# A two-layer encoder on one core: the first norm completed ahead of the projections, and projection tiles convolved straight from PSUM

## The chip, the cores and the metric

One core of a Trainium2 chip runs the whole program. The metric is the time of one execution in microseconds on the device; lower is better. The kernel before was timed three times: median 1426.7 us, from 1426.19 to 1429.39.

## What is computed

The reference is a trunk of two layers over 528 positions (16 learned tokens and 512 inputs) of width 1024. Both layers have the same shape: norm, mixer, norm, residual.

```python
for i in range(DEPTH):                       # DEPTH = 2
    y = rmsnorm(h, norm_pre[i])              # x * rsqrt(mean(x*x) + 1e-6) * gain
    y = hyena_mixer(...) if i == 0 else diff_attention_mixer(...)
    h = h + rmsnorm(y, norm_post[i])
return h[:, 16:]

def hyena_mixer(h, ...):                     # layer 0, inner width E = 2048
    u = h @ w_in + b_in                      # 1024 -> 4 * 2048: x0, x1, v and the gate z
    x0, x1, v = split(dwconv_centred(u[..., :3 * E], conv_w, conv_b))   # three taps
    h_fwd, h_bwd = hyena_filters(...)        # a small sine net, then 64 -> 2 * 2048
    v = bidir_long_conv(v * x1, h_fwd, h_bwd, skip)
    return (v * x0 * silu(u[..., 3 * E:])) @ w_out
```

Layer 1 is differential attention with 16 heads. Everything is float32; a product of two float32 matrices is made of three products of a rounded high part and the rest (high by high, high by low, low by high).

## The kernel before

**Layout.** Activations lie transposed, 1024 channels as 8 blocks (`KT`) of 128 partitions by 528 positions. `xh` and `xl` hold the high and low parts of the normed input of a layer. A weight tile (`wtile`, L325) is loaded in two halves of 128x512 through three buffers `wr`; for each half ScalarE writes the high part `wh` (L209) and VectorE or GpSimd the low part `wl` (L212).

**Layer 0.** Its 2048 channels go in 8 chunks of 256. In a chunk there are eight projection tiles (`in_tile`, L487): v, x1, v, x1, then x0, z, x0, z. A tile is 48 matmuls of 264 columns (`project`, L338: 8 blocks, three products, two halves of the positions). Beside them stand the filters (`filters`, L596: for each chunk `taps`, `tap_sums` and `tap_transform` twice), which need the three-layer sine net `filter_net` (L581) to be complete, then for each chunk the long convolution (`long_conv`, L713) and eight tiles of the output projection (`out_tile`, L855; `out_half` for the last two chunks).

**The first norm.** In `first_load` (L448) `xh` and `xl` are made from x times gain, without the norm's factor, so that projections may start at once. The squares are summed over the blocks on VectorE (L465), then over partitions on TensorE (L270), the root is made on VectorE (L220 to L231), and `first_norm` spreads the 528 factors over all partitions as `rb0`. Each projection tile is multiplied by `rb0` as it leaves PSUM (L504), into a tile `u`, from which ScalarE makes the centre tap (L519) and VectorE the two others (L520, L521).

**PSUM.** Pool `psB` has five banks and `psP` three. A projection tile, two outputs of a filter transform (`tap_transform`) take two banks of `psP`; all else, the out tiles too, takes `psB`.

**What sets the order.** A list of steps (`Filler`) hands out projection and out tiles between the pieces of the filters and convolutions, and a list scheduler of the framework then fixes the order on each engine. Each engine runs its queue strictly in order. All loads go through the queue of SP.

## Time and profile before

| what | value |
|---|---|
| median of three runs | 1426.7 us |
| the profiled execution | 1425.88 us, its span 1424.1 us |
| TensorE busy | 1334.7 us, 94% of the span |
| VectorE busy | 1092.5 us, 77% |
| ScalarE, GpSimd busy | 737.6 us (52%), 568.8 us (40%) |
| mean granted TensorE clock | 0.974 |

The program runs through four stretches: the opening (first loads, first norm, sine net) to about 71 us, the filters to about 194 us, the convolutions to about 690 us, and then the second norm and the attention layer. Time that an engine sits idle counts only where another waits for it; with TensorE at 94%, the stretches where it is not dense are the ones to look at.

### The profile page before, as it was taken

How to read it: one execution, taken by the hardware profiler on the slowest of the kernel's cores; microseconds unless marked ns; L12 is line 12 of the kernel's file. 1: busy time of each engine (PE TensorE's matmuls, PEld its weight loads, DVE VectorE, ACT ScalarE, POOL GpSimd, SP SyncE). 2: the span in 40 equal slices, each digit the busy share in tenths (PEclk: the TensorE clock that was granted, in tenths of full speed). 3: DMA queues.
4: the chain of work that ended last, by engine and by line, in shares of the span. 5: the costliest groups of instructions: out<-in, count | busy, mean ns of one | idle time of the engine just before them, and what ended most of it. 6: DMA issues, size and time to landing. Idle time of an engine off the chain costs nothing. (4 is left out here: it accounts for less than half of the span.)

```text
span 1424.1 us, 24660 instructions
## 1 busy us (share of the span) xinstructions
PE 1334.7 (94%) x9296; PEld 1242.8 (87%) x9296; DVE 1092.5 (77%) x1972; ACT 737.6 (52%) x1415; POOL 568.8 (40%) x678
## 2 busy tenths in 40 slices
PE   5989999999999999999888999999999999899994
PEld 4888899999999999999887788897979889797983
DVE  8889988877777777767778676868678676867877
ACT  5455433443323232323447678665677666567662
POOL 7367634532323232322534244433444443344334
PEclk7999999999999999999988999999999999999997
DMA  5443442232323232323321412212121221212211
GB/s 188 135 138 123 148 153 75 75 119 75 104 75 104 74 105 69 102 72 97 111 61 34 133 46 75 63 42 80 40 89 60 72 68 39 75 45 89 90 67 59
DMA packets 63558, 123.47 MB, mean 87 GB/s; under 512 B 7296, under 2 KB 11648, under 8 KB 63440
## 3 DMA queue, kind: packets, MB, share of 16 engines
q1 hardware_dynamic: 63440, 121.91, 26.3%
q8 instruction: 73, 1.20, 0.4%
q14 instruction: 45, 0.37, 0.1%
HBM read 109.30 MB, written 12.58 MB: 86 GB/s over the span
## 5 line engine op out<-in xcount | busy, mean ns | idle before, releaser
L209 ACT CAST wh<-wr 128x512 fp32r<-128x512 f32 x314 | 182.1, 618 | 238.6 <-PE b L350 66.7
L350 PE MATMUL b<-xl,wh 128*128 128x264 f32 x1024 | 263.3, 289 | 4.8 <-DVE xl L460 4.8
L350 PE MATMUL b<-xh,wh 128*128 128x264 f32 x1024 | 264.9, 291 | 2.5 <-DVE ho L710 0.9
L350 PE MATMUL b<-xh,wl 128*128 128x264 f32 x1024 | 258.6, 289 | 0.8 <-POOL wl L212 0.8
L212 DVE TENSOR_TENSOR wl<-wr,wh 128x512 fp32r<-128x512 f32 x250 | 185.9, 774 | 34.9 <-ACT wh L209 33.4
L350 PEld LDWEIGHTS b<-xh,wh 128*128 128x128 f32 x1024 | 183.9, 193 | 6.3 <-DVE u L504 1.5
L350 PEld LDWEIGHTS b<-xl,wh 128*128 128x128 f32 x1024 | 183.7, 192 | 6.5 <-DVE xl L460 6.1
L350 PEld LDWEIGHTS b<-xh,wl 128*128 128x128 f32 x1024 | 181.6, 192 | 1.3 <-POOL wl L212 1.1
L212 POOL TENSOR_TENSOR wl<-wr,wh 128x512 fp32r<-128x512 f32 x64 | 94.9, 1500 | 62.0 <-ACT wh L209 61.9
L347 PE MATMUL b<-xh,wh 128*128 128x512 f32 x232 | 93.2, 402 | 6.9 <-DVE acc L1266 6.9
L1323 DVE TENSOR_REDUCE mx<-a 128x1 f32<-128x528 f32 x128 | 88.7, 699 | 9.7 <-PE a L1320 8.9
L347 PE MATMUL b<-xh,wl 128*128 128x512 f32 x232 | 91.7, 395 | 0.0
L347 PE MATMUL b<-xl,wh 128*128 128x512 f32 x232 | 91.6, 395 | 0.0
L1266 DVE SCALAR_TENSOR_TENSOR acc<-b,rh,acc 128x512 f32<-128x512 f32 x96 | 70.8, 743 | 22.8 <-PE b L1251 21.9
L516 POOL TENSOR_SCALAR u<-vecs 128x1 f32<-128x1 f32 x96 | 26.4, 296 | 151.6 <-DVE cv L521 129.5
L1329 POOL COPY pp<-pp 128x80 f32<-128x80 f32 x64 | 16.5, 257 | 166.5 <-DVE pp L1328 143.1
L1181 POOL TENSOR_TENSOR ro<-ro,rope 128x528 f32<-128x528 f32 (+1 forms) x32 | 43.2, 1350 | 79.2 <-ACT ro L1170 78.8
L1203 PE MATMUL b<-wh,xh 128*128 128x256 f32 x256 | 73.8, 288 | 0.4 <-DVE vl L1213 0.4
L1203 PE MATMUL b<-wl,xh 128*128 128x256 f32 x256 | 72.6, 284 | 0.0
L1203 PE MATMUL b<-wh,xl 128*128 128x256 f32 x256 | 72.3, 282 | 0.0
L212 DVE TENSOR_TENSOR pl<-b,ph 128x512 fp32r<-128x512 f32 x64 | 43.7, 685 | 33.2 <-ACT ph L209 32.5
L1317 PE MATMUL a<-ks,qs 128*128 128x264 f32 x256 | 55.2, 298 | 10.0 <-ACT qs L209 6.2
(391 smaller groups left out, 4027.3 us busy)
## 6 DMA issues: line engine op xcount, KB each, us to landing
wr<-in_w_in SPq DMA_DIRECT2D x128, 256.0 KB, 2.8
wr<-in_w_out SPq DMA_DIRECT2D x64, 256.0 KB, 2.8
hsp<-ho SPq DMA_DIRECT2D x16, 512.0 KB, 2.7
H<-hsp SPq DMA_DIRECT2D x16, 512.0 KB, 3.9
wr<-in_w_k SPq DMA_DIRECT2D x32, 256.0 KB, 2.7
wr<-in_w_q SPq DMA_DIRECT2D x32, 256.0 KB, 2.7
wr<-in_w_z SPq DMA_DIRECT2D x32, 256.0 KB, 2.7
wr<-in_w_v SPq DMA_DIRECT2D x32, 256.0 KB, 2.6
```

The source lines that it names most:

```text
L209: self.nc.scalar.copy(dst, src)
L212: (eng or self.nc.vector).tensor_tensor(dst, src, hi.bitcast(F32), op=ALU.subtract)
L347: te.matmul(ps, w[:, wk], x[:, k, first:T], start=st, stop=sp)
L350: te.matmul(ps[h], w[:, wk], x[:, k, h * TH:(h + 1) * TH], start=st, stop=sp)
L516: g.tensor_scalar(u[:, e:e + 1], b_in[:, mt:mt + 1], -1.0, None, op0=ALU.mult)
L1181: g.tensor_tensor(y, y, rope[:, 1, n0:n0 + n], op=ALU.mult)
L1203: te.matmul(ps[:n, :256], x, wv[k // 4][w][:, wk], start=(k == 0 and q == 0), stop=(k == KT - 1 and q == len(ops) - 1))
L1266: self.nc.vector.scalar_tensor_tensor(y, ps, r, y, op0=ALU.mult, op1=ALU.add)
L1317: te.matmul(pss[mp][:, h, :TH], qs[:, mp, tq], ks[:, mp, h * TH:(h + 1) * TH], start=True, stop=False)
L1323: v.tensor_reduce(mx, ps[:, :, :TH], axis=AX.XY, op=ALU.max, negate=True)
L1329: self.nc.gpsimd.tensor_copy(view(p, 0, [META, 5], [1, META]), view(p, MR - META, [0, 5], [1, META]))
```

## The change

Three things are done in the code. The first norm is completed before any projection: the squares of each block are summed over partitions on TensorE as they come (`sums`), the root is made with a power on GpSimd (`mhalf`), and each block is then scaled, rounded to `xh` and its rest written to `xl`, in a fixed order. The first two weight tiles are split on VectorE, and two projection tiles are worked on side by side. Projection tiles, now already normed, are convolved directly out of PSUM: `u`, `rb0` and the 264-column products are gone, six fixed tiles `cv` with a column of padding at each end take their place, and a small addition on GpSimd mends the two end columns. PSUM is cut into `psB` with four single banks and `psP` with two pairs; out tiles move to `psP`, and are added to the accumulator in one instruction of 528 columns. A halving of one tap row (L670) moves into a constant. The title of the change also speaks of the second layer's weights, split where they are used; the diff has no line for that, and on all five engines the instructions of the attention layer stand in the same order as before (the last 3641 of TensorE, 800 of VectorE, 699 of ScalarE, 330 of GpSimd, 188 of SP).

```diff
-        self.psB = px.enter_context(tc.tile_pool(name="ps0", bufs=5, space=PSUM))
-        self.psP = px.enter_context(tc.tile_pool(name="ps1", bufs=3, space=PSUM))
+        self.psB = px.enter_context(tc.tile_pool(name="ps0", bufs=4, space=PSUM))
+        self.psP = px.enter_context(tc.tile_pool(name="ps1", bufs=2, space=PSUM))
...
+            items[1], items[2] = items[2], items[1]
...
+                    xts, sums, net = self.first_load(pf, fill)
+                    layers = self.filter_net(pf, hs, net)
+                    next(layers)
+                    with tc.high_priority(offset=400):
+                        last = self.first_norm(pf, xts, sums)
...
+                    with tc.issue_after(last[0]), tc.issue_after(last[1]):
+                        fill.upto(4)
+                        for _ in layers:
+                            fill.upto(fill.at + 2)
+                        self.tables(pf, vb, nb, ib, hb)
...
     def first_load(self, pf, fill):
...
+        for i in (0, 1):
+            fill.fetch(i, nc.vector)
+        for k, xt in enumerate(xts):
             sq = self.tl(pf, [P, T], F32, "sqk", bufs=4)
             nc.scalar.activation(sq, xt, AF.Square)
+            for j in range(6):
+                nc.tensor.matmul(sums[:88, j:j + 1], sq[:, j * 88:j * 88 + 88], self.ones[:, 0:1],
+                                 start=k == 0 and j == 0, stop=k == KT - 1 and j == 5)
...
+    def first_norm(self, pf, xts, sums):
+        v, s, m = self.nc.vector, self.nc.scalar, 88
+        a, y, q, r = [self.tl(self.small, [P, 8], F32, t)[:m, :6] for t in ("rs_a", "rs_y", "rs_q", "rms")]
+        v.tensor_scalar(a, sums[:m, 0:6], 1.0 / D, 1e-6, op0=ALU.mult, op1=ALU.add)
+        self.nc.gpsimd.tensor_tensor(y, a, self.mhalf[:m, :6], op=ALU.pow)
+        v.scalar_tensor_tensor(q, y, -0.5, y, op0=ALU.mult, op1=ALU.mult)
+        v.tensor_tensor(q, q, a, op=ALU.mult)
+        v.scalar_tensor_tensor(r, q, 1.5, y, op0=ALU.add, op1=ALU.mult)
+        rb = self.tl(pf, [P, T], F32, "rb0")
         for h in (0, 1):
             ps = self.tl(self.psB, [P, 512], F32, "b")
+            self.rows(r, 3 * h, 3, m, ps[:, :TH])
+            s.copy(rb[:, h * TH:(h + 1) * TH], ps[:, :TH])
+        keep = self.tc.keep_in_program_order
+        for k in range(KT + 1):
+            if k < KT:
+                xt, xh = xts[k], self.xh[:, k]
+                keep(v.scalar_tensor_tensor(xt, xt, self.gains[:, 0, k:k + 1], rb, op0=ALU.mult, op1=ALU.mult))
+                cast = keep(s.copy(xh, xt))
+            if k:
+                low = keep(v.tensor_tensor(self.xl[:, k - 1], xts[k - 1], self.xh[:, k - 1].bitcast(F32), op=ALU.subtract))
...
     def in_tile(self, pa, b_in, cw, cb2, c, idx, wt, res, part):
...
+            res["ps", idx] = self.tl(self.psP, [P, 2, 512], F32, "b")
...
-                v.tensor_tensor(dst[:, sl], ps[h], self.rb0[:, sl], op=ALU.mult)
...
-        for e in (0, T + 1):
-            g.tensor_scalar(u[:, e:e + 1], b_in[:, mt:mt + 1], -1.0, None, op0=ALU.mult)
-        scaled(u[:, 1:T + 1])
-        s.activation(y, u[:, 1:T + 1], AF.Identity, bias=cb2[:, mt:mt + 1], scale=cw[:, 1, mt:mt + 1])
-        v.scalar_tensor_tensor(y, u[:, 0:T], cw[:, 0, mt:mt + 1], y, op0=ALU.mult, op1=ALU.add)
-        v.scalar_tensor_tensor(y, u[:, 2:T + 2], cw[:, 2, mt:mt + 1], y, op0=ALU.mult, op1=ALU.add)
+        s.activation(at(1), ps, AF.Identity, bias=cb2[:, mt:mt + 1], scale=cw[:, 1, mt:mt + 1])
+        for o in (2, 0):
+            v.scalar_tensor_tensor(at(o), ps, cw[:, 2 - o, mt:mt + 1], at(o), op0=ALU.mult, op1=ALU.add)
+        g.tensor_tensor(ends, ends, self.edge[:, mt], op=ALU.add)
...
-                v.tensor_scalar(pm[0:1, 0], pm[0:1, 0], 0.5, None, op0=ALU.mult)
...
     def out_tile(self, c, st, ws, dt):
-        pss = [self.tl(self.psB, [P, 512], F32, "b")[:, :TH] for _ in (0, 1)]
+        pair = self.tl(self.psP, [P, 2, 512], F32, "b")[:, :, :TH]
...
+            nc.vector.tensor_tensor(ya, ya, pair, op=ALU.add)
```

In numbers of instructions: VectorE loses 128 products of 264 columns (L504), 40 of its 80 out-tile additions (two of 264 become one of 528), 7 sums of squares and 8 halvings, and gains 6 weight splits and 8 subtractions (the 8 scaled rests become 8 scalings and 8 subtractions). GpSimd loses 96 single-column instructions and 6 splits and gains 48 end-column additions. TensorE gains 46 small products. The order on the engines moves at three places.

**VectorE, the first norm.** Before, the root (`rs_a`) stands behind the last sum of squares `sqk`, between two sine layers (`sa`, `sk`):

```order
L465 TENSOR_TENSOR sqk_148<-sqk_148,sqk_199 128x528
L535 TENSOR_SCALAR sa_235<-b_231,net_131 64x264
L465 TENSOR_TENSOR sqk_148<-sqk_148,sqk_206 128x528
L538 TENSOR_SCALAR sk_236<-sa_235 64x528
L212 TENSOR_TENSOR wl_451<-wr_452,wh_450 128x512
L539 TENSOR_SCALAR sk_236<-sk_236 64x528
L220 TENSOR_SCALAR rs_a_254<-b_247 88x6
```

Now the root stands directly behind the split of the fourth weight half (`wr_179`), and the scaled blocks `xt` and rests `xl` follow:

```order
L559 TENSOR_SCALAR sa_252<-sa_252 64x528
L213 TENSOR_TENSOR wl_174<-wr_179,wh_173 128x512
L483 TENSOR_SCALAR rs_a_263<-b_143 88x6
L485 SCALAR_TENSOR_TENSOR rs_q_265<-rs_y_264 88x6
L486 TENSOR_TENSOR rs_q_265<-rs_q_265,rs_a_263 88x6
L487 SCALAR_TENSOR_TENSOR rms_266<-rs_q_265,rs_y_264 88x6
L497 SCALAR_TENSOR_TENSOR xt_144<-xt_144,vecs_82,rb_75_272 128x528
L497 SCALAR_TENSOR_TENSOR xt_146<-xt_146,vecs_82,rb_75_272 128x528
L500 TENSOR_TENSOR xl_84<-xt_144,xh_83 128x528
```

The root has come ahead of the second sine layer, but behind four weight splits, and every projection is now behind it.

**VectorE, where the first projection tile is emptied.** In the change this is `b_315`, read by L533; it stands behind the eighth rest, three weight splits and the start of the second sine layer (`sa`, `sk`):

```order
L500 TENSOR_TENSOR xl_84<-xt_161,xh_83 128x528
L549 TENSOR_SCALAR sa_439<-b_434,net_148 64x264
L549 TENSOR_SCALAR sa_439<-b_435,net_148 64x264
L213 TENSOR_TENSOR wl_366<-wr_367,wh_365 128x512
L213 TENSOR_TENSOR wl_366<-wr_371,wh_365 128x512
L213 TENSOR_TENSOR wl_476<-wr_477,wh_475 128x512
L552 TENSOR_SCALAR sk_440<-sa_439 64x528
L553 TENSOR_SCALAR sk_440<-sk_440 64x528
L533 SCALAR_TENSOR_TENSOR cv_12_103<-b_315,vecs_82,cv_12_103 128x528
L558 SCALAR_TENSOR_TENSOR sa_439<-sk_440,sa_439 64x528
L213 TENSOR_TENSOR wl_476<-wr_481,wh_475 128x512
L533 SCALAR_TENSOR_TENSOR cv_12_103<-b_315,vecs_82,cv_12_103 128x528
```

The third projection tile takes the pair of banks of `b_315`, so TensorE comes to it only after the last of these rows. On ScalarE the casts of the two filter tables `hb0h` and `hb1h` stand just ahead of the first reading of `b_315` (L531), and GpSimd splits these tables (`hb0l`, `hb1l`) as soon as they are cast.

**VectorE, out tiles of a chunk.** Before, the additions to `acc` come in pairs, two single banks for each tile (two tiles shown, and the next split `gl`):

```order
L819 SCALAR_TENSOR_TENSOR y_4807<-v_737_4298,vecs_82,y_4807 128x528
L212 TENSOR_TENSOR gl_4776<-y_4759,gh_4775 128x528
L870 TENSOR_TENSOR acc_2281<-acc_2281,b_4843 128x264
L870 TENSOR_TENSOR acc_2281<-acc_2281,b_4844 128x264
L870 TENSOR_TENSOR acc_2281<-acc_2281,b_4859 128x264
L870 TENSOR_TENSOR acc_2281<-acc_2281,b_4860 128x264
L212 TENSOR_TENSOR gl_4824<-y_4807,gh_4823 128x528
```

Now one addition for a tile, with pieces of the convolution's end (`y`, `gl`) between them:

```order
L822 SCALAR_TENSOR_TENSOR y_5469<-b_5454,rnt_120,zt_5467 128x264
L823 SCALAR_TENSOR_TENSOR y_5469<-b_5454,rnt_120,zt_5467 128x256
L824 SCALAR_TENSOR_TENSOR y_5469<-b_5454,rnt_120,zt_5467 128x8
L830 TENSOR_REDUCE rd_5480<-cr_5478 128x16
L831 TENSOR_TENSOR y_5469<-y_5469,rd_5475 128x16
L883 TENSOR_TENSOR acc_2243<-acc_2243,b_5489 128x528
L831 TENSOR_TENSOR y_5469<-y_5469,rd_5480 128x16
L213 TENSOR_TENSOR gl_5438<-y_5421,gh_5437 128x528
L832 SCALAR_TENSOR_TENSOR y_5469<-v_740_4984,vecs_82,y_5469 128x528
L883 TENSOR_TENSOR acc_2243<-acc_2243,b_5503 128x528
L883 TENSOR_TENSOR acc_2243<-acc_2243,b_5517 128x528
L213 TENSOR_TENSOR gl_5486<-y_5469,gh_5485 128x528
```

On TensorE the last six out tiles of a chunk (72 matmuls) now stand in one run with two pairs of banks between them.

## Rows read from the trace of the kernel before

**Rows 1.** The page: span, busy time of each engine, 40 slices of TensorE.

```profile
span 1424.1 us, 24660 instructions
PE 1334.7 (94%) x9296; PEld 1242.8 (87%) x9296; DVE 1092.5 (77%) x1972; ACT 737.6 (52%) x1415; POOL 568.8 (40%) x678
PE   5989999999999999999888999999999999899994
```

**Rows 2.** Windows (us; busy of PE, PEld, DVE, ACT, POOL, clock): opening, filters, convolutions.

```profile
0.00:20.00 20.00, 9.87 (x35) 7.32 (x36) 15.34 (x26) 13.91 (x23) 13.25 (x23) 0.91 0.84 293
20.00:40.00 20.00, 12.15 (x59) 10.84 (x58) 18.76 (x29) 5.34 (x9) 12.31 (x5) 0.66 0.34 111
...
96.00:196.00 100.00, 92.01 (x715) 88.33 (x714) 92.04 (x142) 49.68 (x92) 64.13 (x62) 1.00 0.44 146
260.00:640.00 380.00, 380.00 (x2987) 373.19 (x2986) 284.68 (x582) 132.43 (x228) 112.20 (x147) 1.00 0.27 88
```

**Rows 3.** DMA of the first 45 us, in 40 slices of 1.125 us.

```profile
GB/s 0 56 314 384 344 372 338 371 369 366 377 375 413 410 253 202 126 142 0 0 0 55 309 102 0 0 0 0 0 15 91 208 267 340 382 257 31 5 0 0
```

**Rows 4.** Timeline of TensorE, opening (start us, us, instruction, idle before).

```profile
30.16 1.92 PE L270 MATMUL b<-ones,sqk 128*88 128x1 f32 x12 [4.95 <-DVE sqk L465]
...
40.01 1.82 PE L286 MATMUL b<-sqk,ones 88*128 88x264 f32 x4 [2.91 <-DVE sqk L280]
...
50.08 0.28 PE L350 MATMUL b<-xh,wh 128*128 128x264 f32 x1
...
52.54 0.29 PE L350 MATMUL b<-xh,wl 128*128 128x264 f32 x1
...
70.95 1.20 PE L660 MATMUL b<-w4h,hs 128*128 128x512 f32 x4 [0.59 <-ACT w4h L209]
```

**Rows 5.** Timeline of VectorE, then GpSimd, while GpSimd splits the filter tables.

```profile
20.43 0.69 DVE L465 TENSOR_TENSOR sqk<-sqk,sqk 128x528 f32<-128x528 f32 x1
21.05 2.89 DVE L460 SCALAR_TENSOR_TENSOR xl<-xt,vecs,xh 128x528 fp32r<-128x528 f32 x1
23.86 2.86 DVE L465 TENSOR_TENSOR sqk<-sqk,sqk 128x528 f32<-128x528 f32 x1
26.65 0.54 DVE L535 TENSOR_SCALAR sa<-b,net 64x264 f32<-64x264 f32 x1
...
19.81 3.56 POOL L212 TENSOR_TENSOR hb0l<-raw,hb0h 128x1024 fp32r<-128x1024 f32 x1 [2.25 <-ACT hb0h L209]
```

**Rows 6.** Timeline of TensorE, then GpSimd: the first filter transform.

```profile
79.08 0.80 PE L703 MATMUL b<-pm,hb0h 128*128 128x256 f32 x2 [4.85 <-ACT pm L209]
79.67 0.42 PE L350 MATMUL b<-xh,wh 128*128 128x264 f32 x1
79.89 0.42 PE L350 MATMUL b<-xl,wh 128*128 128x264 f32 x1
...
84.07 0.41 PE L703 MATMUL b<-pm,hb0h 128*128 128x256 f32 x1
...
79.10 1.69 POOL L212 TENSOR_TENSOR pm<-pm,pm 128x512 fp32r<-128x512 f32 x1 [0.88 <-ACT pm L209]
```

**Rows 7.** Groups by line and shape (busy us, mean ns, idle before), whole span.

```profile
L504 DVE TENSOR_TENSOR u<-b,rb 128x264 f32<-128x264 f32 x96 | 38.2, 423 | 23.9 <-PE b L350 23.6
L520 DVE SCALAR_TENSOR_TENSOR cv<-u,vecs,cv 128x528 f32<-128x528 f32 x48 | 37.3, 777 | 1.2 <-ACT cv L519 0.9
L663 DVE TENSOR_TENSOR pm<-b,dec 128x512 f32<-128x512 f32 x32 | 20.5, 679 | 4.4 <-PE b L661 3.5 <-DMA dec<-in_decay 0.7
L819 DVE SCALAR_TENSOR_TENSOR y<-v,vecs,y 128x528 f32<-128x528 f32 x16 | 13.4, 840 | 0.0
L1266 DVE SCALAR_TENSOR_TENSOR acc<-b,rh,acc 128x512 f32<-128x512 f32 x96 | 70.8, 743 | 22.8 <-PE b L1251 21.9
L1395 POOL TENSOR_TENSOR rh<-vv,mhalf 128x4 f32<-128x4 f32 x15 | 17.0, 1136 | 1.2
```

**Rows 8.** Line L670: duration ns min/median/max, first and last start.

```profile
L670 DVE TENSOR_SCALAR pm<-pm x8: 280/1185/1290, 77.1 to 183.8; 1x256 f32<-1x256 f32 x8
```

More of the change, by code (lines that the diff above doesn't have):

```diff
@@ L57, in shape_constants @@
     hbas = np.stack([np.cos(sg), np.sin(sg)]).transpose(3, 0, 1, 2, 4)
+    hbas[0, 0, 0, 0] *= 0.5
     def rot(tt):
@@ L374, in hyena @@
             cb2 = self.tl(k0, [P, 48], F32, "cb2")
-            self.rb0 = self.tl(k0, [P, T], F32, "rb0")
+            edge = self.edge = self.tl(k0, [P, 48, 2], F32, "edge")
+            self.cv = [self.tl(pa, [P, T + 2], F32, f"cv{i}", bufs=1) for i in range(6)]
+            self.cv_at = 0
+            for t in self.cv:
+                g.memset(view(t, 0, [T + 1, 2]), 0.0)
             vb = [self.tl(k0, [P, 2, 2, 256], F32R, "vbh"), self.tl(k0, [P, 2, 2, 256], F32R, "vbl")]
@@ L419, in hyena @@
                     g.tensor_tensor(cb2, cb2, cb, op=ALU.add)
-                    layers = self.filter_net(pf, hs, net)
-                    for _ in (0, 1):
-                        next(layers)
-                    self.first_norm(pf, self.rb0, part)
-                    fill.fetch(2, g)
-                    fill.upto(4)
-                    for _ in layers:
-                        fill.upto(fill.at + 2)
-                    self.tables(pf, vb, nb, ib, hb)
+                    for i in (0, 1):
+                        g.tensor_tensor(edge[:, :, i], cw[:, 2 * i], b_in[:, 0:48], op=ALU.mult)
+                    g.tensor_scalar(edge, edge, -1.0, None, op0=ALU.mult)
+                    self.load(dtl, I["dtail"])
+                    with tc.issue_after(last[0]), tc.issue_after(last[1]):
[3 more added lines that the diff above has]
+                        self.tables(pf, vb, nb, ib, hb)
                 self.filters(fpool("pl"), hs, hb, dtl, rnt, dpf, dpb, hsp, lambda us: fill.run(us, first[1]))
@@ L450, in first_load @@
         nc = self.nc
-        part = []
+        sums = self.tl(self.psB, [P, 512], F32, "b")
+        xts = []
         for k in range(KT):
@@ L454, in first_load @@
             self.load(xt, self.I["xT"][:, k])
-            if k == 0:
+            xts.append(xt)
+            if k == 1:
+                net = self.net_load(pf)
+            if k == 5:
                 self.load(self.vecs, self.I["vecs"])
-                fill.fetch(0, nc.gpsimd)
-            gain = self.gains[:, 0, k:k + 1]
-            nc.scalar.activation(self.xh[:, k], xt, AF.Copy, scale=gain)
-            nc.vector.scalar_tensor_tensor(self.xl[:, k], xt, gain, self.xh[:, k].bitcast(F32), op0=ALU.mult,
-                                           op1=ALU.subtract)
+        for i in (0, 1):
+            fill.fetch(i, nc.vector)
@@ new lines, in first_load @@
+        return xts, sums, net
+    def first_norm(self, pf, xts, sums):
[7 more added lines that the diff above has]
+        rb = self.tl(pf, [P, T], F32, "rb0")
@@ L476, in first_norm @@
         for h in (0, 1):
             ps = self.tl(self.psB, [P, 512], F32, "b")
-            self.spread(dg[:, h * TH:(h + 1) * TH], ps[:, :TH])
-            self.nc.scalar.copy(rb[:, h * TH:(h + 1) * TH], ps[:, :TH])
+            self.rows(r, 3 * h, 3, m, ps[:, :TH])
[8 more added lines that the diff above has]
+                low = keep(v.tensor_tensor(self.xl[:, k - 1], xts[k - 1], self.xh[:, k - 1].bitcast(F32), op=ALU.subtract))
@@ L481, in in_items @@
+        return cast.ins, low.ins
     def in_items(self, pa, b_in, cw, cb2, c, kinds, res):
@@ L696, in tap_transform @@
         ho = self.tl(ph, [P, 4, 256], F32, "ho", bufs=2)
-        ps = [self.tl(self.psP, [P, 512], F32, "b") for _ in (0, 1)]
+        ps = self.tl(self.psP, [P, 2, 512], F32, "b")
         for a in (0, 1):
@@ L857, in out_tile @@
         gs = st["g"]
-        pss = [self.tl(self.psB, [P, 512], F32, "b")[:, :TH] for _ in (0, 1)]
+        pair = self.tl(self.psP, [P, 2, 512], F32, "b")[:, :, :TH]
+        pss = [pair[:, h] for h in (0, 1)]
         sls = [slice(0, TH), slice(TH, T)]
@@ L864, in out_tile @@
                                      start=(i == 0 and q == 0), stop=(i == 1 and q == 2))
-        for ps, sl in zip(pss, sls):
-            ya = self.yacc[:, dt, sl]
-            if c == 0:
-                nc.scalar.copy(ya, ps)
-            else:
-                nc.vector.tensor_tensor(ya, ya, ps, op=ALU.add)
+        ya = self.yacc[:, dt].rearrange("p (h t) -> p h t", h=2)
+        if c == 0:
+            nc.scalar.copy(ya, pair)
+        else:
+            nc.vector.tensor_tensor(ya, ya, pair, op=ALU.add)
     def boundary(self, pa, pb):
```

46 lines of the change are left out of this document (14 added, 32 removed).

## The prediction

> **What bounds the kernel now.** I read the page first: TensorE is busy 94% of the span, and its slices are thin at the start, near the middle and at the end [rows 1]. Then the windows by stage. From 260 to 640 us TensorE is busy 380.00 of 380.00 us while VectorE has 95 us to spare [rows 2]: there only TensorE's own work sets the time, and the change leaves its large matmuls as they are. In the filters, 96 to 196 us, TensorE is busy 92.01 and VectorE 92.04 of 100 us: both are nearly full, and TensorE loses 8 us to waits. In the first 40 us TensorE is busy 22 us, and at a granted clock of 0.91 and 0.66, so much of it at the 1.2 GHz level [rows 2]. Last the timelines, for who waits there: TensorE stands still 4.95 us for the sums of squares and 2.91 us for the spread factors [rows 4], and 4.85 us ahead of the first filter transform [rows 6]. So the change can earn only before about 196 us, and can lose anywhere.
>
> **The sum** is made against the profiled execution, 1425.88 us, which lies 0.8 us under the median of 1426.7. A measurement of this kernel can tell about 0.2%, 2.85 us, from no change.
>
> *Projections (L504 and its kin).* 128 products of 0.42 us leave VectorE, 54 us in all [rows 7]. Of these, 12 lie in the filters (5.0 us); most others lie where TensorE is full and earn nothing. Their readers L533 take 528 columns from PSUM; the nearest row from PSUM is L1266, 743 ns for 512 columns, so 0.77 us, as L520 now [rows 7]. No cost, no gain.
>
> *Opening.* The loads run at about 370 GB/s from 2.2 us on [rows 3]. Now the eight slices of x, the net and the vectors come first, and the fourth weight half behind one more table and the two filter tables: 5.08 MB, so it lands near 16 us. Its cast and split take 1.3 us, and the root waits behind them in VectorE's queue: 17.5 us. Then the power on GpSimd (1.14 us by L1395, [rows 7]), three short instructions (I take 0.6 us together), twelve passes on TensorE (1.92 us for twelve before, [rows 4]) and a copy: 22 us. Sixteen instructions of 0.7 us [rows 5], all needed in turn, end at 33.3 us. TensorE follows with two tiles at once, 96 matmuls; at the slow pitch of 0.22 us [rows 6] for some 5 us and then the fast one of 0.123 (20 matmuls from 50.08 to 52.54 us, [rows 4]), and never ahead of the rests, it has done them by about 37 us. That is 22 more matmuls than now by 40 us, and it would be a gain of some 5 us.
>
> But then comes the third tile, and it needs the banks of the first. On VectorE eleven rows stand ahead of their release, 6.9 us by their lengths (0.54 twice, five splits or sine steps at 0.7, two at 0.45, two readings at 0.77): 40.2 us. And just then GpSimd splits the filter tables. Before, the two VectorE instructions that met these splits took 2.89 and 2.86 us where their like take 0.7, while the one that read PSUM took 0.54 [rows 5]. I add 2 x 2.15 = 4.3 us: the third tile starts at 44.5 us. The bound below is none, if the splits come a little later than the release; above, a third table split brings 2.15 more. The Trainium skill ("SBUF — State Buffer", "Who interferes with whom") gives a reason: VectorE and GpSimd share a port pair which whichever starts first holds for its whole instruction. These rows agree for the held side; by that rule GpSimd could as well be the one that waits, and then the 4.3 us are nothing.
>
> TensorE has stood still 7 us by then. After its 4.85 us pause it went on at 0.22 us a matmul for 5.5 us [rows 6], so I take the slow level again: 25 matmuls in 5.5 us, then 183 at 0.123 us (22.5 us). The first taps follow 304 matmuls instead of 288, at 72.5 us: **+1.6 us** against 70.95 [rows 4].
>
> *The first filter transform* comes 9.9 us after the taps now (70.95 to 80.8, the end of the third split of `pm`, [rows 4, 6]); L670 leaves that chain, 1.26 us at its slot there. So 8.6 us after 72.5 is 81.1 us; now the transform runs on steadily from 84.07 [rows 6]. That is 3.0 us earlier, and 336 projection matmuls are done by then, not 310: 26 x 0.123 = 3.2 us less left to do in the filters. Together **-6.2 us**, in which the +1.6 of the opening is contained.
>
> *The rest of the filters.* VectorE loses the 5.0 us and eight L670; of these 0.28 us each are certain (the shortest) and 1.19 likely the most (the median), 2.2 to 9.5 us [rows 8]. Of its 92 us it sheds 7 to 14.5. TensorE can gain no more than the 8 us of idle time it has [rows 2]. It also waits for casts and for GpSimd, which are not lightened, so I take **-3 us**, between 0 and -8.
>
> *Out tiles.* The cover of the old five single banks goes. An out tile is 12 matmuls, 1.48 us; with two pairs the next but one waits for the addition of 0.7 us (528/512 of L663, [rows 7]). Between the first and second addition of the run of six, VectorE has a rest `gl` and a skip product, 0.84 us each [rows 7]. I count from the start of that run: 1.5 us of `y` pieces, first addition at 2.3, `gl` and skip until 4.0, second addition done at 4.8; the fourth of these tiles could start at 4.44 and gets its banks at 4.9. A second wait of 0.1 follows. So 0.6 us in each of five chunks (the sixth to eighth do otherwise): **+3 us**. Below it is 0, if VectorE runs ahead; above, one more instruction of 0.84 us in the way of two tiles, 2.3 us a chunk, 11 us.
>
> *At nothing.* GpSimd's 48 end-column additions replace 96 single columns, off any path. The second layer: no instruction moves, as its queues read the same. The second norm's reloads of x go into `cv` tiles which are free some 25 us before they are read.
>
> Sum: -6.2 - 3 + 3 = -6.2 us, 1419.7 us by the profile, 1420.5 by the median. I say **1420.5 us**.
>
> **The rivals.**
> *A. The opening pays in full.* The splits of the tables come after the release or wait themselves (the rule above allows it), TensorE's pause is 3 us and not 7, and it may keep its 2.4 GHz level: -4.3 and about -2.5 more, with the filters at their full 8 us and no wait in the out tiles. 1405 to 1414 us. For it: the queue of VectorE is short of work from PSUM there. Against: the queue order puts both table casts directly ahead of the first reading of `b_315`, as the rows of the change show.
> *B. It cancels.* The filters stay as long as they were, for TensorE's 8 us of waits are for casts as much as for VectorE, and the out tiles eat the rest: -6.2 + 0 + 5 gives 1425.5 us by the median. Against: VectorE at 92% and all waits on it shorten.
> *C. Slower: the two pairs of banks.* If VectorE comes to each addition one instruction later than I count, TensorE waits 2.3 us in each of five chunks and at two of the 30 projection tiles that stand behind one another: +11 to +14 where TensorE has no slack at all (380.00 of 380.00, [rows 2]). -6.2 - 3 + 14 gives +4.8, 1431.5 us. It decides from 2 us a chunk on. For it: five single banks were there to hide just that. Against: VectorE is busy 75% there and loses 0.85 us a tile.
> *D. The change does not do what it says.* For the second layer's weights it does nothing; that is in the sum at 0, and moves no other case.
>
> **How the numbers follow.** My forecast, 1417 to 1425 us, has 0.45; in most of it the gain can be told (0.40), at its edge not (0.05). A has 0.15, B 0.17, C 0.23. So faster 0.40 + 0.15 = 0.55, same 0.05 + 0.17 = 0.22, slower 0.23. The range reaches from 1411 us, into A, to 1430 us, into C, and leaves out about 0.1 at either end.
>
> **What would show it.** Right: the first projection near 23 us, a pause of TensorE of 4 to 8 us ahead of the third tile with VectorE instructions of 2 to 3 us in it, first taps at 71 to 75 us, the first transform at 80 to 83 us, the last transform some 8 to 10 us earlier than 194 us, and waits of TensorE on the out-tile addition of about 0.6 us a chunk. The second layer's length should not move. Wrong: no pause ahead of the third tile (A), a filter stretch of the old 110 us from first to last transform (B), TensorE under 378 of 380 us in the convolutions by many short waits (C), or a difference behind 800 us, for which I have no cause.

## The result and the profile after

The changed kernel takes 1445.97 us (median of 4 runs, 1443.98 to 1450.67); the kernel before took 1426.45 us beside it. The ratio is 1.0139, with a 95% interval of 1.0109 to 1.0170: **slower by 1.4%**, outside the range of the forecast. The profiled execution took 1443.98 us, its span is 18.1 us longer than that of before.

The page after, beside [rows 1] (span, busy time, 40 slices of TensorE):

```profile
span 1442.2 us, 24627 instructions
PE 1353.8 (94%) x9388; PEld 1261.5 (87%) x9388; DVE 1031.9 (72%) x1794; ACT 733.3 (51%) x1407; POOL 544.2 (38%) x634
PE   8889997999999999999898899999999999999994
```

VectorE did lose 60.6 us of work. But TensorE, with the same large matmuls, is busy 19 us longer, and a dent stands in its seventh slice from 216 us on, where [rows 1] has 9. The windows after, beside [rows 2] (us; busy of PE, PEld, DVE, ACT, POOL; clock, DMA share, GB/s); then the same stretch of the kernel before:

```profile
0.00:20.00 20.00, 15.85 (x99) 14.63 (x99) 7.88 (x20) 9.34 (x15) 4.39 (x23) 1.00 0.79 281
20.00:40.00 20.00, 17.64 (x111) 16.15 (x112) 14.47 (x25) 9.75 (x16) 2.68 (x2) 1.00 0.06 19
96.00:196.00 100.00, 93.32 (x696) 89.72 (x695) 82.91 (x127) 51.57 (x96) 65.98 (x60) 0.96 0.44 146
240.00:260.00 20.00, 12.28 (x62) 11.07 (x62) 15.71 (x33) 5.44 (x10) 9.97 (x10) 0.66 0.00 0
260.00:640.00 380.00, 380.00 (x2959) 371.60 (x2959) 247.19 (x452) 125.33 (x214) 104.11 (x117) 1.00 0.27 87
```

```profile
240.00:260.00 20.00, 19.14 (x143) 18.02 (x142) 19.09 (x36) 7.30 (x12) 11.19 (x13) 1.00 0.26 80
```

The first reading is the fourth row: 12.28 of 20 us at a granted clock of 0.66, and 62 matmuls where before ran 143. The filters (third row) show the other loss: VectorE sheds 9 us of 92, TensorE is busy as long as before, but with 19 matmuls fewer, at 0.96 and not 1.00. The timeline of TensorE after, at the places of the prediction (start us, us, what, idle before):

```profile
9.70 10.72 PE L475 MATMUL b<-ones,sqk 128*88 128x1 f32 x72
22.78 2.83 PE L292 MATMUL b<-ident,rms 88*128 88x88 f32 x12 [2.37 <-DVE rms L487]
...
27.55 1.25 PE L351 MATMUL b<-xh,wh 128*128 128x264 f32 x4
...
47.41 0.78 PE L351 MATMUL b<-xh,wh 128*128 128x264 f32 x2 [6.68 <-DVE cv L533]
...
85.05 0.58 PE L716 MATMUL b<-pm,hb0h 128*128 128x256 f32 x1 [1.70 <-POOL pm L213]
...
89.60 0.58 PE L716 MATMUL b<-pm,hb0h 128*128 128x256 f32 x1 [2.27 <-DVE pm L213]
...
247.41 1.25 PE L877 MATMUL b<-gh,wh 128*128 128x264 f32 x4 [5.92 <-ACT gh L210]
249.75 0.81 PE L877 MATMUL b<-gl,wh 128*128 128x264 f32 x2 [1.09 <-DVE gl L213]
```

The pause of 6.68 us ahead of the third tile is the one that was forecast (7). The first taps come at 75.98 us, the first transform begins at 82.97 and runs steadily only from 89.60 us, where before did so from 84.07 [rows 6]. The last transform starts at 200.8 us (193.9 before), the last matmul of the out tiles at 734.2 (710.4 before).

What VectorE did ahead of the wait that ends at 89.60 us; then the last of these instructions, the fourth split of `pm`, in the kernel before:

```profile
84.13 0.69 DVE L677 TENSOR_TENSOR pm<-b,dec 128x512 f32<-128x512 f32 x1 [1.54 <-DMA dec<-in_decay]
...
85.20 2.36 DVE L213 TENSOR_TENSOR wl<-wr,wh 128x512 fp32r<-128x512 f32 x2
87.48 0.75 DVE L533 SCALAR_TENSOR_TENSOR cv<-b,vecs,cv 128x528 f32<-128x528 f32 x1
88.16 1.39 DVE L213 TENSOR_TENSOR pm<-pm,pm 128x512 fp32r<-128x512 f32 x1
```

```profile
79.99 1.35 DVE L212 TENSOR_TENSOR pm<-pm,pm 128x512 fp32r<-128x512 f32 x1 [0.35 <-ACT pm L209]
```

What VectorE and GpSimd did in the pause, and GpSimd and ScalarE in the hole:

```profile
37.67 4.07 DVE L213 TENSOR_TENSOR wl<-wr,wh 128x512 fp32r<-128x512 f32 x3
41.66 2.56 DVE L552 TENSOR_SCALAR sk<-sa 64x528 f32<-64x528 f32 x1
44.26 0.43 DVE L553 TENSOR_SCALAR sk<-sk 64x528 f32<-64x528 f32 x1
44.61 0.75 DVE L533 SCALAR_TENSOR_TENSOR cv<-b,vecs,cv 128x528 f32<-128x528 f32 x1
...
38.67 2.52 POOL L213 TENSOR_TENSOR hb0l<-raw,hb0h 128x1024 fp32r<-128x1024 f32 x1 [16.62 <-ACT hb0h L210]
41.14 2.80 POOL L213 TENSOR_TENSOR hb1l<-raw,hb1h 128x1024 fp32r<-128x1024 f32 x1
...
244.30 1.15 POOL L827 TENSOR_TENSOR cr<-dpb,v 128x256 f32<-128x256 f32 x1 [8.40 <-DVE rd L830]
245.41 1.29 POOL L835 TENSOR_TENSOR y<-y,G 128x528 f32<-128x528 f32 x1
...
246.73 0.63 ACT L210 CAST gh<-y 128x528 fp32r<-128x528 f32 x1 [4.64 <-POOL v L539]
```

In the hole TensorE has finished the inverse transform of chunk 0 at 241.5 us and waits for what follows from it: the pieces of `y`, their correction, the gate, the cast `gh`. The kernel before has that chain too, but its TensorE did projections meanwhile. In the change the out tiles of chunk 0 take the same rotating pairs of banks as the projections, and a rotating pool gives its tiles out in the order in which the program asks for them: the second half of chunk 1's projections, then the out tiles of chunk 0, then the first half of chunk 2's. When the first of these groups is done, the next allowed work is the out tiles, and those wait for `gh`. Of the 16 projection tiles ahead of them, 14 (672 matmuls) are done before the first transposition of the first convolution; two are left to fill its time. The windows of the projections alone (us; busy of PE and PEld; clock, DMA share, GB/s), after and then before:

```profile
236.00:274.70 38.70, 0.00 (x0) 0.00 (x0) 0.82 0.11 38
```

```profile
236.00:274.70 38.70, 25.23 (x188) 23.45 (x186) 1.00 0.26 83
```

In the change not one projection runs from the end of the 16th tile to the last out tile of chunk 0; in the kernel before 188 of their matmuls do.

### The profile page after: what moved, and what is told of

Same layout as the page of the kernel before. It is cut to its first block, busy times and chain, and to the rows that moved or that the text cites. A ratio compares the mean times of both kernels' runs of the same rounds, so it can differ in the third digit from the quotient of the medians.

```text
span 1442.2 us, 24627 instructions
## 1 busy us (share of the span) xinstructions
PE 1353.8 (94%) x9388; PEld 1261.5 (87%) x9388; DVE 1031.9 (72%) x1794; ACT 733.3 (51%) x1407; POOL 544.2 (38%) x634
## 3 DMA queue, kind: packets, MB, share of 16 engines
q8 instruction: 74, 1.21, 0.4%
## 5 line engine op out<-in xcount | busy, mean ns | idle before, releaser
L213 DVE TENSOR_TENSOR wl<-wr,wh 128x512 fp32r<-128x512 f32 x256 | 189.1, 768 | 114.4 <-ACT wh L210 113.9
L351 PE MATMUL b<-xh,wh 128*128 128x264 f32 x1024 | 212.0, 288 | 8.6 <-DVE cv L533 7.0
L351 PE MATMUL b<-xl,wh 128*128 128x264 f32 x1024 | 212.1, 288 | 0.0
L351 PE MATMUL b<-xh,wl 128*128 128x264 f32 x1024 | 208.8, 284 | 0.0
L351 PEld LDWEIGHTS b<-xh,wh 128*128 128x128 f32 x1024 | 160.5, 191 | 12.2 <-ACT vbh L210 6.9
L351 PEld LDWEIGHTS b<-xl,wh 128*128 128x128 f32 x1024 | 161.1, 190 | 0.3
L351 PEld LDWEIGHTS b<-xh,wl 128*128 128x128 f32 x1024 | 160.3, 190 | 0.3
L213 POOL TENSOR_TENSOR wl<-wr,wh 128x512 fp32r<-128x512 f32 x58 | 85.4, 1489 | 58.4 <-ACT wh L210 58.3
L535 POOL TENSOR_TENSOR cv<-cv,edge 128x2 f32<-128x2 f32 x48 | 11.2, 232 | 197.0 <-DVE cv L533 190.8
L533 DVE SCALAR_TENSOR_TENSOR cv<-b,vecs,cv 128x528 f32<-128x528 f32 x96 | 73.2, 762 | 1.1
```

The costliest lines, as they stand in the source:

```text
L213: (eng or self.nc.vector).tensor_tensor(dst, src, hi.bitcast(F32), op=ALU.subtract)
L351: te.matmul(ps[h], w[:, wk], x[:, k, h * TH:(h + 1) * TH], start=st, stop=sp)
L533: v.scalar_tensor_tensor(at(o), ps, cw[:, 2 - o, mt:mt + 1], at(o), op0=ALU.mult, op1=ALU.add)
L535: g.tensor_tensor(ends, ends, self.edge[:, mt], op=ALU.add)
```

## The experiments

Ratios are to the kernel before, run beside it on the same chip; runs that were taken apart from each other are set side by side by their ratios. How far single profiled executions may be compared, four of them tell: the changed kernel and the first three runs below have the same instructions in the same order on all four compute engines up to the first transposition of the first convolution, and reach it at 213.1, 210.4, 210.5 and 209.4 us. Differences of up to 3.7 us by then are no effect of an edit.

**Out tiles of all chunks in singles.** In `out_tile`, and the additions by halves as before:

```diff
-        pair = self.tl(self.psP, [P, 2, 512], F32, "b")[:, :, :TH]
-        pss = [pair[:, h] for h in (0, 1)]
+        pss = [self.tl(self.psB, [P, 512], F32, "b")[:, :TH] for _ in (0, 1)]
```

> The out tiles of a chunk go back to two single banks of the four-bank pool, read by halves, everything else as changed. Theory 1 (the out tiles of chunk 0 now take the rotating pairs in program order, ahead of the projections of chunk 2, so TensorE has nothing else to do when it waits for the gated rows): the projections move up, the idle stretch at 241 to 247 us goes, TensorE is busy 19 of 20 us in 240 to 260, time about 1432 us (1429 to 1435). Rival (GpSimd's products G in front of y*G make the chain longer, whatever the banks): TensorE still waits 5 us or more for gh there, 1443 to 1447 us. Second rival (five single banks were needed, four stall it): the hole goes but TensorE is under 435 of 443 us busy from 265 to 708, 1437 to 1443 us.

1435.31 us, ratio 1.0043 (1.0026 to 1.0060): 13.7 us of the 19.8 us come back.

```profile
240.00:260.00 20.00, 17.60 (x133) 17.34 (x132) 18.90 (x40) 7.38 (x14) 12.03 (x13) 0.91 0.17 53
```

TensorE is busy 17.60 of these 20 us, not the 19 that were expected, as one wait of 2.40 us for a reading (`cv`) is left at 251 us. The hole goes; theory 1 holds, with a time a little above its range.

**Only the order of the list.** The banks stay as changed:

```diff
-                if c > 0:
-                    items += whole(outs[c - 1])
                 if c + 1 < NCH:
                     items += vx(c + 1)
+                if c > 0:
+                    items += whole(outs[c - 1])
```

> Out tiles stay in the pairs of banks; only the order in which the list of filling work is written changes: the projections of the next chunk stand ahead of the out tiles of the last one. Theory 1 (the order in which the pairs are taken is the cause): the idle stretch at 241 to 247 us goes as in the run with single banks, 1429 to 1435 us. Rival (it is the kind and number of banks, not the order): nothing changes, 1443 to 1447 us.

1443.13 us, 1.0092 (1.0070 to 1.0115). The hole goes (17.61 of 20 us), so the order is its cause; but the time falls by only 6.7 us, which neither side had expected. The waits of TensorE in this run, 300 to 700 us (total, times, longest), tell why:

```profile
PE b L877 <- DVE acc L883: 5.1, 5, 1.0
```

The out tiles of a chunk now stand in one run, and one of them waits 1.0 us for the addition, once in each of five chunks: the wait of the prediction's out-tile term, which the changed kernel itself doesn't have (380.00 of 380.00 us). The last matmul of the out tiles starts at 727.5 us, 7.1 behind the run with singles; 5.1 of them are these waits.

**Chunk 0 alone in singles.** `pss` from `psB` if `c == 0`, else the pair:

> Only the out tiles of chunk 0 go to two single banks of the four-bank pool; those of chunks 1 to 5 stay in the pairs. Theory 1 (the one hole at the end of chunk 0 is the loss, and the pairs cost nothing behind it): the hole at 241 to 247 us goes, TensorE stays busy 400 of 400 us from 300 to 700, and the time is 1 to 4 us below that of the run with all out tiles in singles, some 3 to 7 us above the kernel before of the same chip, ratio 1.002 to 1.005. Rival (the hole moves to the end of chunk 1, where the out tiles of chunk 1 are again ahead of the next projections): a new wait for gh of over 4 us near 330 us, ratio 1.009 or more. Second rival (with the hole gone, the second out tile of a run waits for the addition of the one before it, as in the run with the other order, 1 us in each of five chunks): ratio 1.007 to 1.009.

1434.09 us, 1.0036 (1.0022 to 1.0050), TensorE 397.68 of 400 us from 300 to 700, the missing 2.3 us by the end of the convolutions. Theory 1 again: by the ratios 14.7 us for one hole. The traces give less: from the first transposition to the last matmul of the out tiles the changed kernel takes 521.1 us, this run 510.2 and the run with all out tiles in singles 510.0, so 11 us. Both values are within the intervals of the ratios.

**That one edit in the kernel before.** Nothing else of the change:

```diff
-        self.psB = px.enter_context(tc.tile_pool(name="ps0", bufs=5, space=PSUM))
-        self.psP = px.enter_context(tc.tile_pool(name="ps1", bufs=3, space=PSUM))
+        self.psB = px.enter_context(tc.tile_pool(name="ps0", bufs=4, space=PSUM))
+        self.psP = px.enter_context(tc.tile_pool(name="ps1", bufs=4, space=PSUM))
...
-        pss = [self.tl(self.psB, [P, 512], F32, "b")[:, :TH] for _ in (0, 1)]
+        pss = [self.tl(self.psP, [P, 512], F32, "b")[:, :TH] for _ in (0, 1)]
```

First the split of the banks alone:

> The kernel before with its eight single banks split 4 and 4, not 5 and 3, and nothing else. Theory 3 (the lost fifth bank is what lengthened the filters, whose taps and sums take five banks in turn): last transform 2 to 4 us later than 184.2 us, time 1429 to 1433 us on a chip where before is 1427. Rival (the filters don't need it; the loss there is a slower clock and waits that begin in the opening): last transform within 1 us, ratio within 0.002 of 1.

1424.53 us, 0.9971 (0.9946 to 0.9997): the fifth bank wasn't needed, and theory 3 falls. The transform that these expectations name starts at 184.4 us (184.2 before), the last of all 1.4 us later than before, in a profiled execution that was the slowest of the ten (1432.67 us). With both edits:

> The kernel before with its eight single banks split 4 and 4, and with one more edit alone: the out tiles take their two banks from the rotating pool of the projections. Nothing of the change's norm, convolution or pairs is in it. Theory 1 (sharing that pool is what opens the hole): an idle stretch of TensorE for gh of 4 us or more behind the inverse transforms of chunk 0, with a lower granted clock behind it, and a time 10 to 15 us above that of the 4 and 4 split alone (ratio to before 0.9971 there): ratio 1.004 to 1.008. Rival (the hole needs the other edits too, such as the one product G of 528 columns in GpSimd's queue): no wait for gh over 1.5 us, ratio 0.995 to 1.000.

1443.59 us, 1.0105 (1.0078 to 1.0131), by 1.3% over the split alone, more than was expected. Its waits from 200 to 300 us, and its windows:

```profile
PE b L863 <- ACT gh L209: 5.9, 1, 5.9
PE b L801 <- DVE zt L778: 2.2, 1, 2.2
PE b L863 <- DVE gl L212: 1.1, 1, 1.1
```

```profile
220.00:240.00 20.00, 15.39 (x91) 13.92 (x89) 13.15 (x22) 5.11 (x9) 6.11 (x6) 0.91 0.30 96
240.00:260.00 20.00, 14.10 (x74) 12.69 (x75) 14.39 (x29) 5.99 (x14) 9.53 (x10) 0.74 0.00 1
```

The same 5.9 and 1.1 us, in a kernel with the old norm and the old convolution. From the first transposition to the last matmul of the out tiles it takes 515.9 us, the split alone 501.8. Sharing the pool is enough.

**The pause of the opening.** Two kernels on the changed one: the casts of the tables behind the second tile's reading (`with tc.issue_after(second): self.tables(...)`), and besides the first tile's readings ahead of the second sine layer.

> The casts of the filter tables, and with them GpSimd's splits, stand behind the first reading of the second projection tile on ScalarE; VectorE's order is word for word the same. Theory 2 (GpSimd's splits double what VectorE does beside them): the three weight splits and the first sine step ahead of the third tile fall from 6.63 to about 2.8 us together, TensorE's pause from 6.68 to about 2.8, first taps at about 72 us, not 76, and the whole 3 to 5 us shorter, 1441 to 1443 us. Rival (VectorE's queue alone is too long): pause over 5.5 us, time 1445 to 1447. Second rival (the opening is made up for later): pause shorter, time within 1.5 us of 1446.

1445.28 us, 1.0120 (1.0097 to 1.0144).

> As the run with late tables, and besides the two VectorE readings of the first projection tile stand ahead of the second sine layer and of the splits for the fourth tile. Theory 2: TensorE's pause ahead of the third tile is about 1 us, the third tile starts at 41 to 42 us, first taps near 69.5 us, the whole 6 to 8 us shorter than the changed kernel, 1438 to 1440 us. Rival (the time of the opening comes back as waits for VectorE in the filters): first taps near 70 but the last transform of the filters no earlier than 199 us and 1443 to 1447 us.

1448.75 us, 1.0143 (1.0123 to 1.0162). In the first, VectorE's three splits take 1.88 us and not 4.07, the step `sk` 0.42 and not 2.56, and the pause is 2.14 us, as theory 2 had it; in the second it is 1.82. But the waits for the next readings, 1.47 and 2.52 us in the first, 3.42 in the second, take its place, and the tables come later. The second run's time rules out the 6 to 8 us of theory 2: there the pause was moved, not removed. The first can't decide: by its ratio it is 2.7 us below the changed kernel, within the noise of the two. The last transforms start at 206.2 and 201.6 us (200.8 without), but the first of these executions was the slowest of its four (1450.57 us). (More projections stand ahead of the taps in both, 328 and 336 and not 304, so the taps' own start says nothing.) VectorE beside the three splits and the step, in the first:

```profile
37.84 1.88 DVE L213 TENSOR_TENSOR wl<-wr,wh 128x512 fp32r<-128x512 f32 x3
39.64 0.42 DVE L554 TENSOR_SCALAR sk<-sa 64x528 f32<-64x528 f32 x1
```

The same question on top of chunk 0's singles, with two single banks for the third tile (`self.psB if (c, idx) == (0, 2)`), and with the four table splits on VectorE (`self.lo(..., g)` becomes `self.lo(...)`):

> As the run with chunk 0's out tiles in singles, and besides the third projection tile of the opening has two single banks and is read by halves, so that it needs no pair of an earlier tile. Theory 2a (banks are what TensorE waits for in the opening): no pause ahead of the third tile, which starts near 40.6 us, a pause of at most 1.5 us ahead of the fourth, the first transform 4 to 6 us earlier, and the time 4 to 6 us below the run with chunk 0's singles alone. Rival 2b (VectorE is the bound of the opening, its queue is full from 37 to 62 us, so the pause only moves to a later tile, as in the two runs with late tables): the idle time of TensorE from 40 to 80 us stays at 5 to 7 us in sum, and the time is within 1.5 us of the run with chunk 0's singles alone.

1438.92 us, 1.0070 (1.0045 to 1.0094): no pause, but the first transform starts at 84.7 and not 82.0 us, and the run is slower than without. Theory 2a falls; the rival had expected the same time, not 0.34% more.

> As the run with chunk 0's out tiles in singles, and besides the splits of the four large tables are done by VectorE (4 more instructions, some 1.3 us each by the length of the 512-column ones) and not by GpSimd. Theory 2b (VectorE bounds the opening, and loses some 2 us to each of GpSimd's splits): VectorE's other instructions from 37 to 62 us all take their usual 0.4 to 0.8 us, it is through with them 3 to 5 us earlier, and the time is 2 to 4 us below the run with chunk 0's singles alone. Rival (the splits cost VectorE as much when it does them itself): within 1 us. Theory 2a (banks): no change of the idle time of TensorE ahead of the third tile beyond 1 us.

1433.80 us, 1.0033 (1.0020 to 1.0046), as chunk 0's singles alone: the time of its rival, that the splits cost VectorE as much when it does them itself; the gain of theory 2b did not come. TensorE still pauses for 5.03 us (4.96 without). That VectorE bounds the opening is not shown by these two, and both still had the pairs.

**The pairs in the filters.** The rotating pool as four singles, everything read by halves:

```diff
-        self.psP = px.enter_context(tc.tile_pool(name="ps1", bufs=2, space=PSUM))
+        self.psP = px.enter_context(tc.tile_pool(name="ps1", bufs=4, space=PSUM))
...
-        ps = self.tl(self.psP, [P, 2, 512], F32, "b")
+        ps = [self.tl(self.psP, [P, 512], F32, "b") for _ in (0, 1)]
```

> As the run with chunk 0's out tiles in singles, but the rotating pool is four single banks again: projections, filter transforms and the later out tiles take two singles and are read by halves (the additions and the readings of VectorE double in number and halve in length). Theory 4 (a filter transform waits for a whole pair, which is free only when VectorE has read both its banks; these waits, up to 2.5 us, also bring TensorE's clock down): TensorE waits at most 1.4 us at a time for ho between 100 and 190 us, the granted clock there stays at 1.00, the last filter transform comes 3 to 5 us earlier, ratio to before 0.999 to 1.002. Rival (the waits are for VectorE's order of work, however the banks are cut): the same waits, and with the longer VectorE work ratio 1.003 to 1.006.

1429.37 us, 1.0002 (0.9989 to 1.0015). The transforms that these expectations name are those on `pm`, the even chunks; the last of these starts 3.4 us earlier (179.3, not 182.6), the last of all at 195.0, not 197.1 us. Both differences are no larger than what single executions differ by; the ratio and the waits decide. TensorE's waits from 90 to 200 us with pairs, then with singles, and the windows of a stretch that has the longest of them:

```profile
PE b L716 <- DVE ho L723: 3.9, 3, 2.5
```

```profile
PE b L719 <- DVE ho L726: 0.4, 1, 0.4
```

```profile
140.00:156.00 16.00, 13.49 (x92) 12.99 (x91) 13.15 (x22) 8.48 (x16) 9.27 (x9) 0.89 0.38 116
```

```profile
140.00:156.00 16.00, 16.00 (x121) 15.28 (x120) 13.94 (x23) 8.62 (x17) 10.20 (x11) 1.00 0.43 146
```

(With singles the longest wait left is one of 3.3 us for a cast, at 188 us, and it too is followed by a lower clock.) Theory 4 holds by the waits and the ratio: a pair is free only when VectorE has read both halves, a transform waits for that, and the wait of 2.5 us costs a second time, as the granted clock falls with it. The edit undoes the pairs of the projections and the later out tiles too, so the 0.34% is for all of them. With singles 121 matmuls run where 92 did, although VectorE has more to read.

**Sums by pairs.** VectorE adds two squares, TensorE sums four tiles and not eight; alone (on chunk 0's singles), then with the singles everywhere:

```diff
+            if k % 2 == 0:
+                even = sq
+                continue
+            nc.vector.tensor_tensor(sq, sq, even, op=ALU.add)
```

> As the run with chunk 0's out tiles in singles, and besides VectorE adds the squares two by two, so that TensorE takes 48 passes for the sums of the first norm and not 96. Theory 5 (the 96 passes at 0.15 us each are what delays the root, not the split of the fourth weight half): sums done near 16.5 us, not 20.4, the root then ends behind that split near 19.5 us, the first projection starts near 24.5 us, not 27.6, and the time is 2 to 3 us below the run with chunk 0's singles alone, ratio 1.001 to 1.002. Rival (the opening's gain is lost in the next wait for VectorE, as with the late tables): first projection 3 us earlier, but the first transform no more than 1 us earlier, and ratio 1.003 to 1.004.

1434.59 us, 1.0038 (1.0023 to 1.0052): the rival's time.

> Chunk 0's out tiles in singles, single banks everywhere, and sums by pairs, the three together. If theories 4 and 5 both hold their gains add: ratio to before 0.996 to 1.000. If only one holds, 1.000 to 1.003; if neither, 1.003 to 1.006.

1425.29 us, 0.9983 (0.9971 to 0.9996), in the range for both theories. The timeline of TensorE in the latter:

```profile
9.83 5.44 PE L479 MATMUL b<-ones,sqk 128*88 128x1 f32 x36 [0.30 <-DVE sqk L477]
19.99 2.83 PE L292 MATMUL b<-ident,rms 88*128 88x88 f32 x12 [4.72 <-DVE rms L491]
...
24.75 1.25 PE L351 MATMUL b<-xh,wh 128*128 128x264 f32 x4
```

The first projection comes 2.7 us earlier alone, 2.8 here. Alone it is lost again, with longer waits for `ho` (one of 3.26 us near 150 us). Without pairs it is kept: the time is 4.1 us below that of the singles everywhere, taken beside it, and the last transform starts at 190.6 and not 195.0 us.

**The opening again, without pairs.**

> As the run of the three together, and besides the third projection tile of the opening takes two banks of the other pool, so that it waits for no earlier tile. Theory 2a (TensorE's pause of 6 us ahead of the third tile costs time, once the filters have no long waits of their own): pause gone, last filter transform 4 to 6 us earlier than 173.3 us, time 4 to 6 us below the three together, ratio 0.994 to 0.996. Rival 2b (VectorE bounds the opening; TensorE waits for the taps instead): idle time of TensorE from 36 to 90 us in sum about as before the edit, last transform within 1.5 us of 173.3, ratio 0.998 to 1.000.

1425.65 us, 0.9977 (0.9959 to 0.9994): no gain. TensorE's waits from 36 to 90 us, in the three together, then with the third tile's own banks:

```profile
PE b L351 <- DVE cv L540: 6.2, 1, 6.2
PE b L723 <- POOL pm L213: 1.2, 2, 0.9
PE b L723 <- ACT pm L210: 0.5, 1, 0.5
```

```profile
PE b L723 <- ACT pm L210: 3.9, 1, 3.9
PE b L608 <- ACT hd L567: 2.6, 1, 2.6
PE b L351 <- DVE cv L540: 0.7, 2, 0.5
```

About 8 us either way: the sine layers and the taps behind them are what is late then. Theory 2a falls again. The two long waits of the second list end on ScalarE, with a sine and a cast of what VectorE has just written; VectorE itself is busy 25.90 of 26 us there (36 to 62 us, third tile with its own banks):

```profile
36.00:62.00 26.00, 22.64 (x153) 21.15 (x152) 25.90 (x36) 13.48 (x23) 15.61 (x9) 0.87 0.50 160
```

These rows fit the rival that VectorE bounds the opening.

> As the run of the three together, and besides VectorE and not GpSimd splits the four large tables. Theory 2b (VectorE bounds the opening and GpSimd's splits hold it up): the first transforms come 2 to 4 us earlier and stay so, ratio 0.995 to 0.997. Rival (what VectorE is spared in waits it pays in work of its own): ratio 0.997 to 0.999.

**1421.95 us, 0.9955 (0.9941 to 0.9970): the fastest kernel of the study, 0.45% under the kernel before.** VectorE splits a table in 1.21 us, most of its other steps stay at their usual lengths, and the first transform starts at 80.65 us, not 81.86. But the last one starts at 191.2, not 190.6, so the 2 to 4 us of theory 2b are not there, though the ratio lies in its range. The last matmul of the out tiles starts at 711.2 us here and at 711.4 in the three together; of the 6.4 us between the two spans 6.2 lie behind it, in the second layer, which no run edits. The run may not be credited to the tables.

## Why the prediction was wrong

Against the profile the forecast was -6.2 us, the profiled executions differ by +18.1 us. The largest failed step is a term that the sum did not have: what the out tiles of chunk 0 hold up once they share the projections' pool. The 24.3 us by steps (the first two are part of the third's 8.5 us; each carries the scatter of single executions):

- *"22 us" for the copy of the factors, first projection near 23 us*: 27.55. The step let the split of the fourth weight half end last, at 17.5 us; it ended at 19.3. What ended last was the sum itself, 96 passes of which 72 took 10.72 us, 0.15 us each, until 20.42 us; I had counted the twelve passes of the rows, not the 84 that are new, though their price stood in [rows 4]. The spread then took 2.83 us and not 1.92. The runs with half the passes start the projections 2.7 and 2.8 us earlier.
- *The pause of 7 us*: 6.68 us, by the way it was worked out, GpSimd's splits among them. The eleven rows add up to 7.0 us, not 6.9. The splits were priced at 4.3 us; they cost 2.19 (three VectorE splits, 4.07 us for 1.88) and 2.14 (`sk`, 2.56 for 0.42). By the Trainium skill ("SBUF — State Buffer", "Who interferes with whom") whichever of the two starts first holds the shared ports, so GpSimd could as well have been the one to wait; here VectorE waited.
- *"the transform runs on steadily", 3.0 us earlier*: 5.5 us later, from 89.60, which is 8.5 us behind the 81.1 of the sum. The taps are 3.5 us of that. The third split of `pm` ends 9.0 us behind them (8.6 in the sum), so this part of the working held. But the sum stopped at the third split. The fourth, on VectorE, ended at 81.3 us before and now at 89.55: its product waited 1.54 us for the load of a decay row, and two weight splits and a projection reading stood ahead of it. So two waits of 1.70 and 2.27 us and the 1.2 GHz level between and behind them (0.57 granted from 84 to 96 us) were no term. With the 26 projections more that stand ahead of it (3.2 us) the balance there is +2.3, not -6.2: 8.5 us.
- *The rest of the filters, -3 us*: +4.4 us. VectorE did shed its load. The term took it that the waits on VectorE shorten with its load; but with pairs each such wait is for two readings and not one, and the longer waits bring the clock down. At the first transposition the change is 3.0 us late (213.1 for 210.1) with 30 projections fewer done (672 for 702), 3.7 us: +6.7 in all. 7.4 us, of which some 3 are scatter, by the runs with the same instructions (209.4 to 210.5 us). Undoing all the pairs is worth 0.34%.
- *Out tiles, +3 us*: none; -3 us. It appeared, 1.0 us in five chunks, only when the list's order was changed. The rival C saw the right pool, but priced the banks' release and not the order in which they are given out.
- *Not in the sum*: the hole behind chunk 0, +17.1 us by the last out tile (23.8 less 6.7): 7.0 us of waits for `gh` and `gl`, 1.0 more in all other waits together, about 4.9 at the lower clock (9.7 us of work from 247.4 to 259 us at nearly twice the pitch), and 1.7 at a second stretch of it, from 713.0 to 716.4 us, which the kernel before does not have; the last 2.5 us I can't place. The hole alone is 11 us by the traces without it, and 1.03% or 14.7 us by the ratios: about half the error. I read the queue of the out tiles of a chunk in the middle, where 72 matmuls stand in a run, and not the one place where what is ahead of them runs out: chunk 0, with two projection tiles left. Between its out tiles and those of chunk 1 stand eight.
- *The second layer, no move*: -5.7 us in these two executions. Its instructions stand in the same order. In the fourteen runs of this study, none of which edits it, the stretch from the last out tile to the end takes 709.1 to 716.8 us (713.7 before, 708.0 after); a difference of 5.7 us is within this scatter of 7.7.

What was right: with the two faults of the banks undone (chunk 0's out tiles and the pairs) the norm and the convolution from PSUM bring the time back to that of the kernel before (1.0002). That they cost nothing is not shown: the split of the banks into 4 and 4 is in that run too, and alone it measured 0.9971 (0.9946 to 0.9997). Nor is a gain from VectorE's lighter load: from the first to the last transform that run takes 108.7 us where before takes 114.8, but 240 projection matmuls stand in between and not 288, which is 5.9 us. It took the sums by pairs as well to come below the kernel before (0.9983). That the opening itself is worth -6 us was not shown.

## What to carry to other kernels

When two kinds of tiles move into one rotating pool, write down the order in which the program asks for them, and look at every place where the next one in turn waits for a long chain: what stands behind it can no longer fill the time, however ready it is. Two pairs of banks did not serve as well here as four single ones: a pair is free only when the last of both has been read. A saving on an engine that others wait for counts only by the waits that end with it; add to each remaining wait what the clock may cost behind it. And run the same code more than once before a few microseconds of one trace are put down to an edit.

## What the hardware showed that was not expected

A wait can cost twice. Behind the 5.92 us of the hole the matmuls of 264 columns follow each other at 0.22 us and not 0.123 until 259 us, and even the single wait of 2.51 us at 148 us (chunk 0's singles) is followed by a granted clock of 0.84 from 150 to 156 us. The waits of 1.3 to 1.95 us in the filters of the kernel before left it at 1.00. But the length of one wait alone doesn't tell: in the changed kernel a wait of 1.37 us that ends at 191.1 us, and three of 0.42, 0.84 and 1.07 us between 709 and 713 us, go with the 1.2 GHz level as well (the clock stands behind the five engines):

```profile
190.70:197.50 6.80, 5.80 (x24) 5.24 (x25) 4.72 (x8) 2.16 (x4) 2.83 (x4) 0.50 0.19 77
713.00:716.40 3.40, 3.40 (x17) 3.40 (x17) 1.52 (x4) 0.85 (x3) 1.28 (x1) 0.51 0.67 197
```

GpSimd's splits of 1024 columns (2.5 to 2.8 us) hold up also a VectorE step with one input: `sk` from 0.42 to 2.56 us. The same split on VectorE takes 1.21 us, less than the delay that it causes from GpSimd (4.33 us for two in the changed kernel). The Trainium skill ("SBUF — State Buffer", "Who interferes with whom") counts such one-input steps among those that can take the shared ports; these rows agree.
